# Matmul with bias and residual: groups of eight tiles in place of four, with one home for each residual group

## The chip, the cores and the metric

The kernel runs on one core of one Trainium2 chip. The metric is the device time of one execution in microseconds (us), the median of three runs. A profile is one more execution, read by a hardware profiler; its span leaves out a little at both ends of the device time.

## The reference

```python
x: 16 x 512 x 1024 f32, weight: 1024 x 768 f32, bias: 768 f32, residual: 16 x 512 x 768 f32
out = np.matmul(x, weight) + bias + residual        # f32
```

Flattened, it is 8192 rows of x, each times the whole weight. The kernel reads 33.6 MB of x, 25.2 MB of residual and 3.1 MB of weight and writes 25.2 MB, 87.04 MB in all.

## The kernel before, in words

**Tiles.** The 8192 rows are cut into 64 tiles of 128 rows. Four tiles (G = 4) are a group of 512 rows, which is loaded and stored with one DMA each. In `group`, partition p holds four consecutive rows of the group, so a partition's share of x is 16 KB in one piece, of residual and output 12 KB; tile j of the group takes row j of every partition. The weight is cut the same way, in two halves of 512 rows with four consecutive rows on a partition, and the strided view in `transpose` picks the columns of x that match.

**One tile's way.** ScalarE (ACT) casts the tile of x to bf16 (`cast_x`, L118; tiles 0 and 2 are shared out between ACT and VectorE, DVE: L115, L116). TensorE (PE) transposes it with eight matmuls against an identity into PSUM (`transpose`, L134). DVE copies the result to SBUF (`copy_xt`, L141). PE multiplies it with the bf16 weight in 16 matmuls, for each of eight k one of 512 and one of 256 columns (`matmul`, L148). `evacuate` ends it: in the first three groups (LATE = 3) DVE adds the bias into an output tile (L163) and GpSimd (POOL) the residual (L164); later DVE adds the product to the residual tile in place (L167) and POOL the bias (L169), and the residual tile is what is stored. The last group's bias is added ahead of time, half on DVE and half on POOL (`add_bias`, L177). The last tile is done in two column chunks (L275, L278).

**Buffers.** Four x slots of 16 KB a partition; a ring of nine slots of 12 KB that the two weight halves, the residual groups and the three output groups take in turn; four slots each for the cast x (`xb`) and the transposed x (`xt`); two PSUM slots for the transposes and three for the products. A load into a slot waits until the last reader of what it held is done; where a residual slot was stored from, it waits for that store to land.

**Order.** Every engine works in the order of the program text (`tc.keep_in_program_order`), and so does SP's queue, which issues all loads and stores (L90, L95, L99, L103): while one waits, all behind it wait. A DMA also waits for the one eight places before it to land, as eight completion semaphores are used in turn. The DMAs in flight share the core's 16 DMA engines and land in the order of issue.

**Start.** SP loads x rows 0 and 1 of the first group, w0, x rows 2 and 3, and the other weight pieces; then x groups 1 and 2, residual 0, x group 3, residuals 1 to 3. PE runs filler matmuls (`fill`, L201) while it waits. Tiles 0 to 2 are multiplied with each k of the weight as it arrives and is cast (`cast_w`, L123 on ACT, L125 on DVE); the bias is spread over the partitions (L212, `stream_shuffle`) before the first of these casts; tile 3 is transposed meanwhile. Its matmuls open the loop over tiles 3 to 62, in which PE transposes tile t + 1 ahead of the matmuls of tile t, and ACT casts tile t + 3. After the fourth tile of each group the loop loads x and residual four groups ahead and stores the group.

Of the kernel before, what the change touches and what calls it, by code (L numbers as in the profile page):

```python
# [8 lines left out]
FP32 = mybir.dt.float32  # L9
BF16 = mybir.dt.bfloat16  # L10
P = 128
G = 4
X_BUFS = 4
RING = 9
XB_BUFS = 4
XT_BUFS = 4
PT_BUFS = 2
PO_BUFS = 3
LATE = 3


@with_exitstack
def kernel(
# [8 lines left out]
    nc = tc.nc  # L32
# [4 lines left out]
    N = weight.shape[1]  # L37
    n_k = K // P
    n_sub = M // P
    n_grp = n_sub // G  # L40
    chunks = [(0, 512), (512, N - 512)]

    def group(ap, g):

        return ap[g * G * P:(g + 1) * G * P, :].rearrange("(p j) k -> p j k", p=P)


    w_dram = weight.rearrange("(h p j) n -> h p j n", p=P, j=4)
# [3 lines left out]
    ring_pool = ctx.enter_context(tc.tile_pool(name="ring", bufs=1))  # L52
# [7 lines left out]
    def o(ins):  # L60
        return tc.keep_in_program_order(ins)
# [3 lines left out]
    def slot(pool, base, n, shape, dtype, name=None):  # L65
        i = count.get(base, 0)
        count[base] = i + 1
        return pool.tile(shape, dtype, name=name or base, tag=f"{base}{i % n}", bufs=1)
# [4 lines left out]
    bias_rows = const.tile([P, N], FP32, name="bias_rows")  # L73
# [7 lines left out]
    w_sb = const.tile([P, n_k, N], BF16, name="w_sb")  # L81
    bias_bc = const.tile([P, N], FP32, name="bias_bc")


    x_tiles, r_tiles, o_tiles, w_stage = {}, {}, {}, {}

    def load_x(g, j0=0, j1=G):
        if g not in x_tiles:
            x_tiles[g] = slot(xin_pool, "x_tile", X_BUFS, [P, G, K], FP32)
        o(nc.sync.dma_start(out=x_tiles[g][:, j0:j1, :], in_=group(x2d, g)[:, j0:j1, :]))  # L90

    def load_w(h, j0, j1):
        if h not in w_stage:
            w_stage[h] = slot(ring_pool, "ring", RING, [P, G, N], FP32, name="w_stage")
        o(nc.sync.dma_start(out=w_stage[h][:, j0:j1, :], in_=w_dram[h, :, j0:j1, :]))  # L95

    def load_r(g):
        r_tiles[g] = slot(ring_pool, "ring", RING, [P, G, N], FP32, name="r_tile")
        o(nc.sync.dma_start(out=r_tiles[g], in_=group(res2d, g)))  # L99

    def store(g, j0=0, j1=G, n0=0, n1=N):
        src = o_tiles[g] if g < LATE else r_tiles[g]
        o(nc.sync.dma_start(out=group(out2d, g)[:, j0:j1, n0:n1], in_=src[:, j0:j1, n0:n1]))  # L103


    xb_tiles, pt_tiles, xt_tiles, po_tiles = {}, {}, {}, {}

    def cast_x(t, split=False):
        if t >= n_sub:
            return  # L110
        xb_tiles[t] = slot(xb_pool, "xb", XB_BUFS, [P, K], BF16)
        src = x_tiles[t // G][:, t % G, :]
        if split:
            h = K // 2
            o(nc.scalar.copy(out=xb_tiles[t][:, :h], in_=src[:, :h]))  # L115
            o(nc.vector.tensor_copy(out=xb_tiles[t][:, h:], in_=src[:, h:]))  # L116
        else:
            o(nc.scalar.copy(out=xb_tiles[t], in_=src))  # L118

    def cast_w(k, act=False):  # L120
        h, j = divmod(k, 4)
        if act:
            o(nc.scalar.copy(out=w_sb[:, k, :], in_=w_stage[h][:, j, :]))  # L123
        else:
            o(nc.vector.tensor_copy(out=w_sb[:, k, :], in_=w_stage[h][:, j, :]))  # L125

    def transpose(t):
        if t >= n_sub:
            return
        xb = xb_tiles.pop(t).rearrange("m (h p j) -> m h j p", p=P, j=4)  # L130
        pt = slot(pt_pool, "pt", PT_BUFS, [P, n_k, P], BF16)
        for k in range(n_k):
            h, j = divmod(k, 4)
            o(nc.tensor.transpose(out=pt[:, k, :], in_=xb[:, h, j, :], identity=ident))  # L134
        pt_tiles[t] = pt

    def copy_xt(t):
        if t >= n_sub:
            return
        xt_tiles[t] = slot(xt_pool, "xt", XT_BUFS, [P, n_k, P], BF16)  # L140
        o(nc.vector.tensor_copy(out=xt_tiles[t], in_=pt_tiles.pop(t)))  # L141

    def matmul(t, k0=0, k1=n_k):
        if t not in po_tiles:
            po_tiles[t] = slot(po_pool, "po", PO_BUFS, [P, N], FP32)
        for k in range(k0, k1):
            for (n0, nl) in chunks:
                o(nc.tensor.matmul(  # L148
                    po_tiles[t][:, n0:n0 + nl],
                    lhsT=xt_tiles[t][:, k, :],  # L150
                    rhs=w_sb[:, k, n0:n0 + nl],
                    start=(k == 0),
                    stop=(k == n_k - 1),
                ))

    def evacuate(t):
        g, j = divmod(t, G)
        po = po_tiles[t]
        if g < LATE:
            if g not in o_tiles:  # L160
                o_tiles[g] = slot(ring_pool, "ring", RING, [P, G, N], FP32, name="o_tile")
            ot = o_tiles[g]
            o(nc.vector.tensor_add(out=ot[:, j, :], in0=po, in1=bias_bc))  # L163
            o(nc.gpsimd.tensor_add(out=ot[:, j, :], in0=ot[:, j, :], in1=r_tiles[g][:, j, :]))  # L164
        else:
            rt = r_tiles[g][:, j, :]
            o(nc.vector.tensor_add(out=rt, in0=po, in1=rt))  # L167
            if g < n_grp - 1:
                o(nc.gpsimd.tensor_add(out=rt, in0=rt, in1=bias_bc))  # L169
        po_tiles.pop(t)  # L170
        xt_tiles.pop(t)

    def add_bias(t):
        g, j = divmod(t, G)
        rt = r_tiles[g]
        engine = nc.gpsimd if j % 2 else nc.vector
        o(engine.tensor_add(out=rt[:, j, :], in0=rt[:, j, :], in1=bias_bc))  # L177


    load_x(0, 0, 2)  # L180
    load_w(0, 0, 1)
    load_x(0, 2, 4)
    load_w(0, 1, 2)
    load_w(0, 2, 4)
    load_w(1, 0, 2)
    load_w(1, 2, 3)
    load_w(1, 3, 4)
    load_x(1)
    load_x(2)
    load_r(0)  # L190
    load_x(3)
    load_r(1)
    load_r(2)
    load_r(3)


    warm_ps = po_pool.tile([P, P], FP32, name="warm_ps", tag="po2", bufs=1)
# [1 line left out]
    def fill(n):  # L199
        for i in range(n):  # L200
            o(nc.tensor.matmul(warm_ps, lhsT=warm_in, rhs=warm_in, start=True, stop=True))  # L201
# [2 lines left out]
    fill(40)  # L204
    cast_x(0, True)
    transpose(0)
    fill(10)
    copy_xt(0)
    cast_x(1)
    transpose(1)  # L210
    fill(6)
    o(nc.vector.stream_shuffle(out=bias_bc, in_=bias_rows, mask=[0] * 32))  # L212
    cast_w(0)
    matmul(0, 0, 1)
    copy_xt(1)
    fill(4)
    matmul(1, 0, 1)
    cast_x(2, True)
    transpose(2)
    cast_w(1)  # L220
    copy_xt(2)
    matmul(0, 1, 2)
    matmul(1, 1, 2)
    matmul(2, 0, 2)
    cast_x(3)
    transpose(3)
    copy_xt(3)
    for k in range(2, 6):
        cast_w(k, k % 2 == 0)
        for t in range(3):  # L230
            matmul(t, k, k + 1)
    cast_w(6)
    cast_w(7, True)
    matmul(0, 6, 7)
    matmul(1, 6, 7)
    matmul(0, 7, 8)
    evacuate(0)
    matmul(2, 6, 8)
    matmul(1, 7, 8)
    evacuate(2)  # L240
    evacuate(1)
    cast_x(4)
    cast_x(5)


    for t in range(3, n_sub - 1):
        g, j = divmod(t, G)
        cast_x(t + 3)
        if t == 3:
            matmul(t)  # L250
            transpose(t + 1)
        else:
            transpose(t + 1)
            matmul(t)
        copy_xt(t + 1)
        evacuate(t)
        if g == n_grp - 2 and j >= 2:
            add_bias(n_sub - G + 2 * (j - 2))
            add_bias(n_sub - G + 2 * (j - 2) + 1)
        if j == G - 1:  # L260
            if g + 4 < n_grp:
                load_x(g + 4)
                load_r(g + 4)
            store(g)
        elif g == n_grp - 1 and j == 1:
            store(g, 0, 2)
        elif g == n_grp - 1 and j == 2:
            store(g, 2, 3)


    t = n_sub - 1
    for (n0, nl) in chunks:
# [4 lines left out]
        rt = r_tiles[n_grp - 1][:, G - 1, n0:n0 + nl]  # L277
# [30 lines left out]
```

## Time and profile before

| | us |
|---|---|
| three runs | 212.57, 212.7, 213.39; median 212.7 |
| the profiled execution | 212.85 |
| its span | 211.1 |
| PE busy (matmuls) | 202.3 (96%) |
| POOL busy | 114.5 (54%) |
| DVE busy | 107.0 (51%) |
| ACT busy | 66.0 (31%) |
| SP's DMA queue | packets take 97.9% of what 16 engines have |

How to read it. The span is that of the profiled execution; 212.85 less 211.1 is what lies around it. A busy share is of the span. The page cuts the span into 40 slices of 5.3 us and gives a digit for each engine, the busy share in tenths. The chain of waits goes back from the last instruction to what released it, and is listed in order of time as start, duration, what. A line of the timeline has start, duration, engine, source line, operation, output <- inputs, shape, count, and in brackets the idle time before it and what ended it.

### The profile page before, as it was taken

Reading aid. Unit: us, or ns where it says so; the run is one execution under the profiler, and the core shown is the slowest. Engines: PE = TensorE matmul, PEld = TensorE weight load, DVE = VectorE, ACT = ScalarE, POOL = GpSimd, SP = SyncE. Lnnn points to the kernel's source line nnn. Section 1 sums busy time; section 2 is a strip of 40 time slices with the busy share of each in tenths; the row PEclk is TensorE's granted clock in tenths of the full one; section 3 lists DMA queues with packets and bytes.
Section 4 is the critical chain, followed back from the end, with each engine's and each line's share of the span. In section 5 each row is a group of like instructions: output and inputs, shape, how many; then the busy total and the mean of one; then the engine's idle time right before and its main releaser. Section 6 shows DMA issues by size and latency. Waiting matters only on the chain.

```text
span 211.1 us, 3768 instructions
## 1 busy us (share of the span) xinstructions
PE 202.3 (96%) x1596; PEld 134.7 (64%) x1596; DVE 107.0 (51%) x142; ACT 66.0 (31%) x69; POOL 114.5 (54%) x69
## 2 busy tenths in 40 slices
PE   8599799999999999999999999999999999999992
PEld 7455466666666666666666666666666666666551
DVE  0664454554455445544554554455445544555942
ACT  2441772312507042150705225070430606033000
POOL 2000019699865565566556655665565566557910
PEclk9999999999999999999999999999999999999999
DMA  6999999999999999999999999999999999999895
GB/s 216 421 436 420 425 432 420 422 438 415 434 412 427 432 425 432 422 434 420 425 428 426 437 417 437 422 425 428 426 432 425 432 420 429 435 419 432 354 416 194
DMA packets 8377, 87.29 MB, mean 414 GB/s; under 512 B 932, under 2 KB 1060, under 8 KB 2216
## 3 DMA queue, kind: packets, MB, share of 16 engines
q1 hardware_dynamic: 8352, 87.04, 97.9%
q8 instruction: 12, 0.20, 0.4%
q14 instruction: 5, 0.04, 0.0%
q10 hardware_dynamic: 8, 0.01, 0.0%
HBM read 61.88 MB, written 25.17 MB: 412 GB/s over the span
## 4 chain that ended last, share of the span: by engine, by line
PE 85%; DMA 10%; DVE 2%; issue 1%; ACT 1%; POOL 0%; ACTq 0%; DVEq 0%; POOLq 0%
PE po L148 72%; PE pt L134 12%; DMA x_tile<-in_x_dram 7%; DMA bias_rows<-in_bias_dram 3%; PE last_ps L275 1%; DVE r_tile L177 1%; ACT xb L118 1%; DVE xt L141 0%; DVE r_tile L278 0%; POOL ident masks.py:197 0%; ACTq L118 0%; POOL bias_rows L74 0%; DVE r_tile L167 0%; DVEq L167 0%; POOLq L292 0%
## 5 line engine op out<-in xcount | busy, mean ns | idle before, releaser
L148 PE MATMUL po<-w_sb,xt 128*128 128x512 bf16 x1008 | 174.6, 326 | 1.2 <-DVE w_sb L125 0.8
L148 PEld LDWEIGHTS <-xt 128*128 128x128 bf16 x1008 | 95.9, 98 | 59.4 <-issue 1.6
L169 POOL TENSOR_TENSOR r_tile<-r_tile,bias_bc 128x768 f32<-128x768 f32 x48 | 88.3, 1840 | 56.0 <-DVE r_tile L167 56.0
L118 ACT CAST xb<-x_tile 128x1024 bf16<-128x1024 f32 x62 | 61.0, 1043 | 115.2 <-DMA x_tile<-in_x_dram 109.2
L167 DVE TENSOR_TENSOR r_tile<-po,r_tile 128x768 f32<-128x768 f32 x51 | 48.8, 957 | 73.6 <-PE po L148 62.9
L141 DVE COPY xt<-pt 128x1024 bf16<-128x1024 bf16 x64 | 43.6, 681 | 4.9 <-PE pt L134 4.8
L134 PEld LDWEIGHTS <-xb 128*128 128x128 bf16 x512 | 35.4, 113 | 10.3 <-ACT xb L118 1.6
L134 PE MATMUL pt<-ident,xb 128*128 128x128 bf16 x512 | 39.1, 219 | 2.4 <-ACT xb L115 1.3
L164 POOL TENSOR_TENSOR o_tile<-o_tile,r_tile 128x768 f32<-128x768 f32 x12 | 21.4, 1822 | 30.3 <-DMA r_tile<-in_residual_dram 30.3
L163 DVE TENSOR_TENSOR o_tile<-po,bias_bc 128x768 f32<-128x768 f32 x12 | 11.3, 955 | 14.5 <-PE po L148 13.0
L201 PE MATMUL warm_ps<-warm_in 128*128 128x128 bf16 x60 | 6.1, 282 | 1.1 <-DVE warm L77 1.1
L201 PEld LDWEIGHTS <-warm_in 128*128 128x128 bf16 x60 | 5.5, 132 | 1.2 <-DVE warm L77 1.1
L123 ACT CAST w_sb<-w_stage 128x768 bf16<-128x768 f32 x3 | 2.5, 833 | 4.2 <-DMA w_stage<-in_weight_dram 4.2
L177 POOL TENSOR_TENSOR r_tile<-r_tile,bias_bc 128x768 f32<-128x768 f32 x2 | 3.6, 1804 | 0.0
L116 DVE CAST xb<-x_tile 128x512 bf16<-128x512 f32 x2 | 0.8, 423 | 5.2 <-DMA x_tile<-in_x_dram 5.2
L177 DVE TENSOR_TENSOR r_tile<-r_tile,bias_bc 128x768 f32<-128x768 f32 x2 | 3.1, 1551 | 0.0
L125 DVE CAST w_sb<-w_stage 128x768 bf16<-128x768 f32 x5 | 2.7, 556 | 0.5 <-DMA w_stage<-in_weight_dram 0.4
L275 PE MATMUL last_ps<-w_sb,xt 128*128 128x512 bf16 (+1 forms) x16 | 2.8, 326 | 0.0
L115 ACT CAST xb<-x_tile 128x512 bf16<-128x512 f32 x2 | 1.2, 618 | 3.9 <-DMA x_tile<-in_x_dram 3.9
L275 PEld LDWEIGHTS <-xt 128*128 128x128 bf16 x16 | 1.6, 98 | 1.1
L78 ACT ACT_TABLE_LOAD x1 | 1.3, 1283 | 2.6 <-POOL ident masks.py:199 2.6
L278 DVE TENSOR_TENSOR r_tile<-last_ps,r_tile 128x512 f32<-128x512 f32 (+1 forms) x2 | 1.1, 559 | 0.9 <-PE last_ps L275 0.8
(12 smaller groups left out, 3.1 us busy)
## 6 DMA issues: line engine op xcount, KB each, us to landing
x_tile<-in_x_dram SPq DMA_DIRECT2D x15, 2048.0 KB, 32.9
r_tile<-in_residual_dram SPq DMA_DIRECT2D x16, 1536.0 KB, 32.1
out_dram<-r_tile SPq DMA_DIRECT2D x12, 1536.0 KB, 31.7
out_dram<-o_tile SPq DMA_DIRECT2D x3, 1536.0 KB, 25.2
x_tile<-in_x_dram SPq DMA_DIRECT2D x2, 1024.0 KB, 6.7
w_stage<-in_weight_dram SPq DMA_DIRECT2D x4, 384.0 KB, 9.7
w_stage<-in_weight_dram SPq DMA_DIRECT2D x2, 768.0 KB, 10.2
out_dram<-r_tile SPq DMA_DIRECT2D x1, 768.0 KB, 5.6
```

The lines of the kernel that those rows point to most:

```text
L118: o(nc.scalar.copy(out=xb_tiles[t], in_=src))
L125: o(nc.vector.tensor_copy(out=w_sb[:, k, :], in_=w_stage[h][:, j, :]))
L134: o(nc.tensor.transpose(out=pt[:, k, :], in_=xb[:, h, j, :], identity=ident))
L141: o(nc.vector.tensor_copy(out=xt_tiles[t], in_=pt_tiles.pop(t)))
L148: o(nc.tensor.matmul(po_tiles[t][:, n0:n0 + nl], lhsT=xt_tiles[t][:, k, :], rhs=w_sb[:, k, n0:n0 + nl], start=(k == 0), stop=(k == n_k - 1),))
L163: o(nc.vector.tensor_add(out=ot[:, j, :], in0=po, in1=bias_bc))
L164: o(nc.gpsimd.tensor_add(out=ot[:, j, :], in0=ot[:, j, :], in1=r_tiles[g][:, j, :]))
L167: o(nc.vector.tensor_add(out=rt, in0=po, in1=rt))
L169: o(nc.gpsimd.tensor_add(out=rt, in0=rt, in1=bias_bc))
L177: o(engine.tensor_add(out=rt[:, j, :], in0=rt[:, j, :], in1=bias_bc))
L201: o(nc.tensor.matmul(warm_ps, lhsT=warm_in, rhs=warm_in, start=True, stop=True))
L275: o(nc.tensor.matmul(ps, lhsT=xt_tiles[t][:, k, :], rhs=w_sb[:, k, n0:n0 + nl], start=(k == 0), stop=(k == n_k - 1)))
```

## The change

- G is 8: one DMA serves eight tiles, and a partition's piece is 32 KB for x and 24 KB for residual and output. There are two x slots of 32 KB in place of four of 16 KB, and four slots of 24 KB (`home`) in place of nine of 12 KB. HOME names the slot of each residual group; slot 0 first holds the whole weight, slot 2 the output of group 0.
- Only group 0 has an output tile of its own, and its residual is loaded later; POOL adds that residual for all eight tiles in a row after tile 12 (`add_residual`). All other groups add in place.
- A table, `moves`, says after which tile SP issues which load and store. The residual and store of a group come later than before, and each x load two groups ahead.
- The start: the first x group comes in five pieces (rows 0-1, 2, 3, 4-5, 6-7), the last three behind the weight, which comes in seven. Tile 2 is cast by ACT alone, tile 3 by ACT and DVE together after the weight; its transposes come after the matmuls of tiles 0 to 2. The bias is spread after the cast of w5. Fills are 40, 8 and 6 in place of 40, 10, 6 and 4. There are five `xb` slots.
- In the loop, tile 3's matmuls are parted by the transposes of tile 4, and tile 7's come before the transposes of tile 8.
- At the end, tiles 61 to 63 get their bias on DVE beforehand, one a tile at tiles 57 to 59; the others up to 60 on POOL after their own add. The last group is stored in pieces of four, two and one tiles and the two chunks of the last tile.

```diff
--- before.py
+++ after.py
@@ -9,14 +9,13 @@
 FP32 = mybir.dt.float32
 BF16 = mybir.dt.bfloat16
 P = 128
-G = 4
-X_BUFS = 4
-RING = 9
-XB_BUFS = 4
+G = 8
+X_BUFS = 2
+HOME = [3, 1, 0, 3, 1, 2, 0, 3]
+XB_BUFS = 5
 XT_BUFS = 4
 PT_BUFS = 2
 PO_BUFS = 3
-LATE = 3
 
 
 @with_exitstack
@@ -81,6 +80,9 @@
     w_sb = const.tile([P, n_k, N], BF16, name="w_sb")
     bias_bc = const.tile([P, N], FP32, name="bias_bc")
 
+    def home(i, name):
+        return ring_pool.tile([P, G, N], FP32, name=name, tag=f"ring{i}", bufs=1)
+
 
     x_tiles, r_tiles, o_tiles, w_stage = {}, {}, {}, {}
 
@@ -90,16 +92,17 @@
         o(nc.sync.dma_start(out=x_tiles[g][:, j0:j1, :], in_=group(x2d, g)[:, j0:j1, :]))
 
     def load_w(h, j0, j1):
-        if h not in w_stage:
-            w_stage[h] = slot(ring_pool, "ring", RING, [P, G, N], FP32, name="w_stage")
-        o(nc.sync.dma_start(out=w_stage[h][:, j0:j1, :], in_=w_dram[h, :, j0:j1, :]))
+        if not w_stage:
+            w_stage[0] = home(0, "w_stage")
+        o(nc.sync.dma_start(out=w_stage[0][:, 4 * h + j0:4 * h + j1, :],
+                            in_=w_dram[h, :, j0:j1, :]))
 
     def load_r(g):
-        r_tiles[g] = slot(ring_pool, "ring", RING, [P, G, N], FP32, name="r_tile")
+        r_tiles[g] = home(HOME[g], "r_tile")
         o(nc.sync.dma_start(out=r_tiles[g], in_=group(res2d, g)))
 
     def store(g, j0=0, j1=G, n0=0, n1=N):
-        src = o_tiles[g] if g < LATE else r_tiles[g]
+        src = o_tiles[g] if g == 0 else r_tiles[g]
         o(nc.sync.dma_start(out=group(out2d, g)[:, j0:j1, n0:n1], in_=src[:, j0:j1, n0:n1]))
 
 
@@ -118,11 +121,10 @@
             o(nc.scalar.copy(out=xb_tiles[t], in_=src))
 
     def cast_w(k, act=False):
-        h, j = divmod(k, 4)
         if act:
-            o(nc.scalar.copy(out=w_sb[:, k, :], in_=w_stage[h][:, j, :]))
+            o(nc.scalar.copy(out=w_sb[:, k, :], in_=w_stage[0][:, k, :]))
         else:
-            o(nc.vector.tensor_copy(out=w_sb[:, k, :], in_=w_stage[h][:, j, :]))
+            o(nc.vector.tensor_copy(out=w_sb[:, k, :], in_=w_stage[0][:, k, :]))
 
     def transpose(t):
         if t >= n_sub:
@@ -154,44 +156,43 @@
                 ))
 
     def evacuate(t):
+
+
         g, j = divmod(t, G)
-        po = po_tiles[t]
-        if g < LATE:
-            if g not in o_tiles:
-                o_tiles[g] = slot(ring_pool, "ring", RING, [P, G, N], FP32, name="o_tile")
-            ot = o_tiles[g]
-            o(nc.vector.tensor_add(out=ot[:, j, :], in0=po, in1=bias_bc))
-            o(nc.gpsimd.tensor_add(out=ot[:, j, :], in0=ot[:, j, :], in1=r_tiles[g][:, j, :]))
+        po = po_tiles.pop(t)
+        if g == 0:
+            o(nc.vector.tensor_add(out=o_tiles[0][:, j, :], in0=po, in1=bias_bc))
         else:
             rt = r_tiles[g][:, j, :]
             o(nc.vector.tensor_add(out=rt, in0=po, in1=rt))
-            if g < n_grp - 1:
-                o(nc.gpsimd.tensor_add(out=rt, in0=rt, in1=bias_bc))
-        po_tiles.pop(t)
+            if t < n_sub - 3:
+                add_bias(t)
         xt_tiles.pop(t)
 
-    def add_bias(t):
-        g, j = divmod(t, G)
-        rt = r_tiles[g]
-        engine = nc.gpsimd if j % 2 else nc.vector
-        o(engine.tensor_add(out=rt[:, j, :], in0=rt[:, j, :], in1=bias_bc))
+    def add_bias(t, engine=nc.gpsimd):
+        rt = r_tiles[t // G][:, t % G, :]
+        o(engine.tensor_add(out=rt, in0=rt, in1=bias_bc))
+
+    def add_residual(t):
+        ot = o_tiles[0][:, t, :]
+        o(nc.gpsimd.tensor_add(out=ot, in0=ot, in1=r_tiles[0][:, t, :]))
 
 
     load_x(0, 0, 2)
     load_w(0, 0, 1)
-    load_x(0, 2, 4)
+    load_x(0, 2, 3)
     load_w(0, 1, 2)
-    load_w(0, 2, 4)
-    load_w(1, 0, 2)
-    load_w(1, 2, 3)
-    load_w(1, 3, 4)
+    load_w(0, 2, 3)
+    load_w(0, 3, 4)
+    load_w(1, 0, 1)
+    load_w(1, 1, 2)
+    load_w(1, 2, 4)
+    load_x(0, 3, 4)
+    load_x(0, 4, 6)
+    load_x(0, 6, 8)
     load_x(1)
-    load_x(2)
-    load_r(0)
-    load_x(3)
     load_r(1)
-    load_r(2)
-    load_r(3)
+    o_tiles[0] = home(2, "o_tile")
 
 
     warm_ps = po_pool.tile([P, P], FP32, name="warm_ps", tag="po2", bufs=1)
@@ -204,68 +205,82 @@
     fill(40)
     cast_x(0, True)
     transpose(0)
-    fill(10)
+    fill(8)
     copy_xt(0)
     cast_x(1)
+    cast_w(0)
     transpose(1)
+    copy_xt(1)
     fill(6)
-    o(nc.vector.stream_shuffle(out=bias_bc, in_=bias_rows, mask=[0] * 32))
-    cast_w(0)
     matmul(0, 0, 1)
-    copy_xt(1)
-    fill(4)
     matmul(1, 0, 1)
-    cast_x(2, True)
+    cast_x(2)
+    cast_w(1)
     transpose(2)
-    cast_w(1)
     copy_xt(2)
     matmul(0, 1, 2)
     matmul(1, 1, 2)
     matmul(2, 0, 2)
-    cast_x(3)
-    transpose(3)
-    copy_xt(3)
     for k in range(2, 6):
         cast_w(k, k % 2 == 0)
         for t in range(3):
             matmul(t, k, k + 1)
+    o(nc.vector.stream_shuffle(out=bias_bc, in_=bias_rows, mask=[0] * 32))
     cast_w(6)
     cast_w(7, True)
-    matmul(0, 6, 7)
-    matmul(1, 6, 7)
-    matmul(0, 7, 8)
+    cast_x(3, True)
+    matmul(0, 6, 8)
     evacuate(0)
+    matmul(1, 6, 8)
     matmul(2, 6, 8)
-    matmul(1, 7, 8)
+    transpose(3)
+    copy_xt(3)
+    evacuate(1)
     evacuate(2)
-    evacuate(1)
     cast_x(4)
     cast_x(5)
 
 
+    moves = {
+        4: [(load_x, 2)],
+        5: [(load_r, 0), (load_r, 2)],
+        12: [(load_x, 3), (load_r, 3)],
+        15: [(store, 1)],
+        20: [(load_x, 4)],
+        21: [(load_r, 4), (store, 0)],
+        28: [(load_x, 5)],
+        29: [(load_r, 5), (store, 2)],
+        36: [(load_x, 6)],
+        37: [(load_r, 6), (store, 3)],
+        44: [(load_x, 7)],
+        45: [(load_r, 7), (store, 4)],
+        47: [(store, 5)],
+        55: [(store, 6)],
+        59: [(store, 7, 0, 4)],
+        61: [(store, 7, 4, 6)],
+        62: [(store, 7, 6, 7)],
+    }
     for t in range(3, n_sub - 1):
-        g, j = divmod(t, G)
         cast_x(t + 3)
         if t == 3:
+            matmul(t, 0, 5)
+            transpose(t + 1)
+            matmul(t, 5, 8)
+        elif t == G - 1:
             matmul(t)
             transpose(t + 1)
         else:
             transpose(t + 1)
             matmul(t)
         copy_xt(t + 1)
+        if n_sub - 7 <= t < n_sub - 4:
+            add_bias(t + 4, nc.vector)
         evacuate(t)
-        if g == n_grp - 2 and j >= 2:
-            add_bias(n_sub - G + 2 * (j - 2))
-            add_bias(n_sub - G + 2 * (j - 2) + 1)
-        if j == G - 1:
-            if g + 4 < n_grp:
-                load_x(g + 4)
-                load_r(g + 4)
-            store(g)
-        elif g == n_grp - 1 and j == 1:
-            store(g, 0, 2)
-        elif g == n_grp - 1 and j == 2:
-            store(g, 2, 3)
+        if t == 12:
+            for u in range(G):
+                add_residual(u)
+        for move, *what in moves.get(t, []):
+            move(*what)
 
 
     t = n_sub - 1
```

## The prediction

> **What bounds the kernel now.** I read the page's slices first, then the chain that ended last, then the timeline of the start and the end, then the landings of single transfers. The slices say that two things are full at once:
>
> ```profile
> PE   8599799999999999999999999999999999999992
> DMA  6999999999999999999999999999999999999895
> PEclk9999999999999999999999999999999999999999
> q1 hardware_dynamic: 8352, 87.04, 97.9%
> PE 85%; DMA 10%; DVE 2%; issue 1%; ACT 1%; POOL 0%; ACTq 0%; DVEq 0%; POOLq 0%
> ```
>
> TensorE and the DMA engines are both at 9 tenths from the second slice to the last but one, at a granted clock of 0.999. The chain of waits tells which ends last:
>
> ```profile
> 21.93 0.04 ACTq L118
> ...
> 24.06 0.64 PE pt L134 x8
> 24.70 2.61 PE po L148 x16
> 27.31 0.45 PE pt L134 x8
> 27.75 2.60 PE po L148 x16
> ...
> 195.79 2.15 DVE r_tile L177
> 197.94 0.61 DVE xt L141
> ...
> 204.42 2.61 PE last_ps L275 x16
> 207.06 0.42 DVE r_tile L278
> ```
>
> From 24.06 on it is TensorE alone, 0.45 + 2.60 us a tile, a period of 3.048 us (tile 5's transposes at 24.06, tile 6's at 27.31, tile 8's matmuls ending at 39.5). Before that the chain is in the second x load, which holds ACT's casts until 22. After PE's end at 207.04 come one add, the last store (issued 207.51, landed 210.0) and the end at 211.07: a tail of 4.03 us. So the time is PE's start, 60 tiles at a fixed pace, and the tail.
>
> The transfers are barely quicker than that. The landings recorded for single transfers step by 4.85 us for 2048 KB of x, 3.66 for a residual, 3.70 for a store: 12.2 us for four tiles, where PE takes 4 x 3.048 = 12.19. The slack of x late in the run:
>
> ```profile
> 188.12 3.89 ACT L118 CAST xb<-x_tile 128x1024 bf16<-128x1024 f32 x4 [8.32 <-DMA x_tile<-in_x_dram]
> ...
> 191.66 0.61 PE L134 MATMUL pt<-ident,xb 128*128 128x128 bf16 x8
> ```
>
> ACT starts the casts of the last group when x lands, and PE transposes the first of these tiles 3.5 us later. The changed kernel must therefore shorten PE's path and must not let the DMA queue run dry by more than a few us.
>
> **The transfers, part by part.** By the recorded packets, 12288 B take 460 ns on an engine (median), 16384 B 611, 6144 B 234, 3072 B 121: 0.0369 ns a byte and 7 to 8 ns a packet. Bytes stay at 87.04 MB. Data packets fall from about 7420 to 4990 (x rows of 32 KB, residual and store rows of 24 KB, but the first x group in five pieces and w in seven), so 2430/16 x 7.4 ns = 1.1 us less for each engine. No row has a 32 KB packet: if packets are cut back to 16 KB and 12 KB it is 0; if all per-packet cost went, 7420/16 x 7.4 = 3.4 us. I take 1.1, since four sizes lie on one line. By it eight tiles take 9.7 + 7.3 + 7.4 = 24.4 us at most, PE 24.38. Nothing of it lies on the path of PE; it moves the end only if the queue ends last.
>
> The Trainium skill's page "DMA: Bandwidth & Descriptors", Anatomy of one DMA, gives a fixed 2.0 us for each DMA beside bytes/436 GB/s; by it 22 DMAs fewer would save up to 44 us, but 1536 KB landing every 3.66 us leaves no room for a fixed part, so I use nothing of it. The same page, Latency and other measured facts, speaks against wide power-of-two pitches (207 GB/s at a row pitch of 512 KiB, 164 at 2 MiB); no run here shows one, x at 16 KB pitch moves at 16 x 16384/611 = 429 GB/s, no slower than 12 KB rows at 427, and the sum has no term for it.
>
> **The start.** The order on SP becomes x rows 0-1, w0, x row 2, w1 to w5, w6-7, then x row 3, 4-5, 6-7, x group 1, residual 1. Up to w6-7 this is 0.52 MB less ahead of the last weights (1.2 us by the 2.4 us between the landings of the first and second 1024 KB of x). Landings, stepping by the same rates from the shown 6.13 (first x): w0 7.2, x row 2 8.4, w1 9.4, w2 10.3, w3 11.3, w4 12.3, w5 13.2, w6-7 15.1. Before shows a slip of 0.8 us at the last weight piece (15.30 to 17.05 for 384 KB, where 0.96 is usual), which I spread: w6-7 15.1 to 15.9, x row 3 16.3 to 17.1, rows 4-5 18.8 to 19.5, rows 6-7 21.2 to 21.9. x group 1 lands at 31.6 and residual 1 at 38.9; these bytes are those of before's 39.27.
>
> PE then: the weight casts (0.56 DVE, 0.83 ACT) end by 16.0 to 16.7, the last two k of tiles 0 to 2 are 12 matmuls of 0.163 = 1.95, to 18.3 (middle). Transposes of tile 3 and copy_xt(3), 0.45 + 0.2 + 0.69, to 19.6; ten matmuls 1.63, tile 4's transposes 0.45, six matmuls 0.98: tile 3 ends at 22.7. Tiles 4 to 6 at 3.05 each: 31.8. Tile 7 is put ahead of tile 8's transposes, as x group 1 lands only at 31.6: 34.4. Then two transposes, a bare wait for copy_xt(8) of 0.45 and 2.6: tile 8 ends at 38.4, 0.75 to 1.45 around it. Before has it at 39.5. **Gain 1.1 us.** The bias spread (1.01 us of DVE), moved from ahead of cast_w(0) to behind w5's cast, is hidden there by the wait for w6-7; without that cover it would cost its 1.0. The fills dropped (6 of 60) run only where PE waits.
>
> **The steady part.** SP's queue is in order, so a waiting instruction holds all behind it. With PE's tile t ending at 38.4 + 3.048(t-8), step by step:
> - x2 waits for the cast of tile 7 (about 24); r0 and r2 follow at once. The queue is full to then. Landings: x2 48.6, r0 55.9, r2 63.2. Tile 16 ends at 62.8, so its add waits 0.4 us; copy_xt(18) behind it on DVE ends at 65.0, needed at 66.3. Residual 1 at 38.9 against tile 8 at 38.4 likewise.
> - x3 waits for the cast of tile 15, which the fifth xb buffer allows at about 38.5: lands 72.9.
> - r3 goes into residual 0's slot, so it waits for eight residual adds that POOL does in a row from 55.9, 1.785 each (10.70/6): 70.3. Behind it on SP wait store 1 and x4. The packets of x3 end at about 71.9 and an issue takes about 1.0 us to its first packet (0.74 to 1.73 at the start): **margin 0.6 us**, no gap. POOL's bias adds of tiles 13 to 15 queue behind: store 1 at 75.9, no gap (r3 lands 80.2).
> - r4 waits for store 1's landing (87.6), r5 for store 0 (112.0), r6 for store 2 (136.4), r7 for store 3 (160.8), each with the next x still 9.7 us in the queue ahead or behind it. x4 to x7 land at 97.3, 121.7, 146.1, 170.5 and are needed at tiles 31, 39, 47, 55, 8 us later; r4 to r7 land 6.8 us ahead.
> So PE is nowhere held; cost 0. By the ledger the queue ends at 207.4; with the two slips of 0.6 and 0.9 us that before's landings show (at 150.8 and 167.4), 208.9 at worst. PE's path has its last store land at 210.0 - 1.2 = 208.8.
>
> **The end.** Three bias adds go to DVE (tiles 61 to 63) where before had two on DVE and two more on POOL.
>
> ```profile
> 195.32 1.81 POOL L177 TENSOR_TENSOR r_tile<-r_tile,bias_bc 128x768 f32<-128x768 f32 x1
> 195.79 2.15 DVE L177 TENSOR_TENSOR r_tile<-r_tile,bias_bc 128x768 f32<-128x768 f32 x1
> ```
>
> A DVE add with two SBUF inputs took 0.95 alone and 2.15 beside a POOL add (it ended 0.81 after POOL did). Three such in three tiles, each waiting for POOL's add, push copy_xt(61) to about 0.15 us past its need; before lost 0.25 there. Bounds: 0 to 0.9 (one more blocked add, 2.15 less 1.25). Gain 0.1.
>
> **Sum.** 212.85 (the profiled execution: span 211.1 and 1.8 around it) - 1.1 - 0.1 = 211.65; the median shown lies 0.15 lower, so **211.5**, its own range 210.6 (1.45 at the start, no stall at the end) to 212.2.
>
> **Rivals.** *The queue ends last*: packets of 32 KB are no cheaper, or the slips are larger. For: the queue's end and PE's are within 0.2 us of each other, and 1.1 us of saving is an extrapolation. Against: 2.97 us of idle, a mean of the 16 engines, between before's first and last packet. Price: queue end 208.9 + 1.1 = 210.0, so 212.7: no change. *SP stands at r3*: POOL's eight residual adds are slower, or residual 0 lands late; the queue drains at 72 with store 1 and x4 stuck behind r3. For: POOL adds of 2.46 and 2.53 stand in the last 20 us of the trace, and residual groups have no slot to spare. Against: those were beside DVE adds of two SBUF inputs, which group 1 has none of. At 2.5 each it is 8 x 0.715 = 5.7 us, less the margin 0.6: the queue ends at 207.4 + 5.1 + 1.5 = 214, 5.2 past PE's store: 216.7. It makes the kernel slower than before once the adds are late by 0.6 + 1.1 = 1.7 us or more (queue end 208.9 against before's 210.0); 2.5 us late gives 212.7 + 0.8 = 213.5. *The start gains nothing*: tile 3, now alone behind the weights, waits for a late x row 3, 1.2 us more: 212.7.
>
> **How the numbers follow.** The forecast 0.50, the queue or the start without gain 0.32, SP at r3 0.18. Something over 0.5% (211.64 to 213.76 around the median) is what a measurement can tell. Most of the forecast's own range lies on the faster side (0.42 of 0.50) and a better packet saving cannot add much, as PE's path stays: faster 0.45; within 0.5% 0.37 (the rest, the second case and a little of the third); slower 0.18. The range leaves out the dearer part of the third case: 210.5 to 214.0.
>
> **What would show it.** Right: tile 8's matmuls end near 38.4; PE's last matmul near 205.8; periods of 3.048 with no gaps at tiles 16, 24, 32; r3 issued near 70 with no drop in the DMA slices there; packets of 32 KB near 1215 ns. Wrong: a dip in the DMA slices at 70 to 76, ACT's casts ending at need at tile 32 or later, a last store that lands long after the last add, or DVE adds of tile 61 to 63 that hold copy_xt by more than 1 us.

## The result

| | median us | runs | range |
|---|---|---|---|
| before | 212.97 | 20 | 212.57 to 213.74 |
| after | 214.03 | 20 | 212.59 to 215.08 |

The ratio after to before is 1.0044, 95% interval 1.0023 to 1.0064: slower by 0.9 us by this ratio (the medians differ by 1.06), where 211.5 was forecast. The times of after are spread over twice the range of before's. The profiled execution of after took 214.12 us, its span is 212.3.

**The profile after.** The page's slices, queue and chain:

```profile
PE   7797999999999999999999999999999999999960
...
PEclk9999999999999999999999999999999999999997
DMA  6999999999999899999999999999999999999993
GB/s 234 405 420 435 482 411 423 448 404 417 435 420 468 324 347 392 448 420 432 431 440 445 411 425 415 445 428 418 440 440 443 401 445 429 423 426 438 408 413 120
...
q1 hardware_dynamic: 5616, 87.03, 97.3%
...
PE 87%; DMA 7%; issue 1%; DVE 1%; ACT 0%; SPq 0%; POOL 0%; POOLq 0%
```

A third of the packets is gone (5616 for 8352), as meant: the data packets among them fall from 7424 to 4992. PE now has nothing to do in the last slice, while DMA is still at 3 tenths: the end has changed hands. And in the slices 14 to 16 (69 to 85 us) the rate falls to 324, 347 and 392 GB/s, although the DMA digit falls only once, to 8. Before has 432, 425 and 432 there:

```profile
GB/s 216 421 436 420 425 432 420 422 438 415 434 412 427 432 425 432 422 434 420 425 428 426 437 417 437 422 425 428 426 432 425 432 420 429 435 419 432 354 416 194
```

The end of the chain of waits after:

```profile
200.05 2.60 PE po L150 x16
202.65 2.61 PE last_ps L290 x16
205.26 0.02 issue
205.29 0.42 DVE r_tile L293
```

PE's last matmul ends at 205.26, before 207.04: PE's path became 1.8 us shorter in this execution. But this chain stops at the last compute instruction. The landing of the last store stands in the list of DMA issues, whose last column is the time from issue to landing. Before, then after:

```profile
out_dram<-r_tile SPq DMA_DIRECT2D x1, 128.0 KB, 2.5
```

```profile
out_dram<-r_tile SPq DMA_DIRECT2D x1, 384.0 KB, 6.8
out_dram<-r_tile SPq DMA_DIRECT2D x1, 256.0 KB, 6.0
out_dram<-r_tile SPq DMA_DIRECT2D x1, 128.0 KB, 5.7
```

Before's last store, 128 KB, landed 2.5 us after its issue, after's 5.7: issued at 205.74, it lands at 211.44. It stood behind other stores. The DMA queue ends last, not PE.

**Where the queue lost time.** SP's part of the timeline of after (start, duration, line, what):

```profile
39.74 0.33 SPq L92 DMA_DIRECT2D x_tile<-in_x_dram  x1
70.58 0.33 SPq L102 DMA_DIRECT2D r_tile<-in_residual_dram  x1
75.91 0.35 SPq L106 DMA_DIRECT2D out_dram<-r_tile  x1
76.35 0.38 SPq L92 DMA_DIRECT2D x_tile<-in_x_dram  x1
```

and the waits of SP's queue:

```profile
SPq L102 <- POOL o_tile L178: 14.3, 1, 14.3
```

From 39.74 to 70.58 SP issues nothing; at the last it stands for 14.3 us at residual 3, for the residual adds of POOL. What it issued then came 2.7 us before x group 3, the last transfer in the queue, had landed (73.27). Residual 3 landed at 83.85, 10.6 us behind x group 3; the other residuals whose landing is recorded take 7.3 to 7.5. After that the steps are again 7.3 and 9.7, but for two slips of 0.6 and 0.8 us, as before had two. The windows view of after at this place (busy time of each engine, then the granted clock, the DMA share and GB/s):

```profile
63.00:71.00 8.00, 7.89 (x59) 5.22 (x60) 4.57 (x6) 1.04 (x1) 8.00 (x6) 1.00 0.93 396
71.00:80.00 9.00, 8.95 (x72) 6.00 (x72) 4.66 (x6) 4.93 (x5) 9.00 (x6) 1.00 1.00 337
80.00:89.00 9.00, 8.89 (x71) 5.94 (x71) 4.66 (x6) 3.14 (x3) 9.00 (x6) 1.00 1.00 424
```

From 71 to 80 the DMA share is 1.00 and the rate 337 GB/s: the engines are not idle, their packets are slow. The recorded packets say which. A packet of 24 KB usually takes 912 ns. On one engine, residual 3 (eight packets) runs 1990, 910, 910, 910, 910, 1010, 2120, 980 ns. Most engines show this: the first packet takes 1.4 to 2.0 us where the engine had run dry before it; on nearly all the seventh takes 1.6 to 2.2, and the sixth or the eighth some tenths too long. Four engines never ran dry, and their eight packets still took 1.5 us over the usual time, the others' 1.9 to 3.0. As a mean of the 16 engines that is 2.0 us, and only 0.3 us of idle. On the slowest engine it is 3.0 us, and a transfer lands with its slowest engine: the step was 3.3 us over the usual.

### The profile page after: what moved, and what is told of

Same layout as the page of the kernel before. It is cut to its first block, busy times and chain, and to the rows that moved or that the text cites. A ratio compares the mean times of both kernels' runs of the same rounds, so it can differ in the third digit from the quotient of the medians.

```text
span 212.3 us, 3674 instructions
## 1 busy us (share of the span) xinstructions
PE 199.6 (94%) x1560; PEld 133.8 (63%) x1590; DVE 110.3 (52%) x143; ACT 66.7 (31%) x69; POOL 111.0 (52%) x68
## 3 DMA queue, kind: packets, MB, share of 16 engines
q1 hardware_dynamic: 5616, 87.03, 97.3%
## 4 chain that ended last, share of the span: by engine, by line
PE 87%; DMA 7%; issue 1%; DVE 1%; ACT 0%; SPq 0%; POOL 0%; POOLq 0%
PE po L150 73%; PE pt L136 13%; DMA x_tile<-in_x_dram 4%; DMA bias_rows<-in_bias_dram 3%; PE last_ps L290 1%; DVE xt L143 1%; ACT xb L118 0%; DVE r_tile L293 0%; SPq L97 0%; POOL ident masks.py:197 0%; POOL bias_rows L73 0%; POOLq L307 0%
## 5 line engine op out<-in xcount | busy, mean ns | idle before, releaser
L150 PE MATMUL po<-w_sb,xt 128*128 128x512 bf16 (+1 forms) x978 | 172.2, 324 | 3.2 <-DVE xt L143 1.5
L174 POOL TENSOR_TENSOR r_tile<-r_tile,bias_bc 128x768 f32<-128x768 f32 x53 | 95.5, 1816 | 85.1 <-DVE r_tile L167 85.0
L167 DVE TENSOR_TENSOR r_tile<-po,r_tile 128x768 f32<-128x768 f32 x55 | 52.6, 956 | 76.1 <-PE po L150 65.8
L178 POOL TENSOR_TENSOR o_tile<-o_tile,r_tile 128x768 f32<-128x768 f32 x8 | 14.2, 1820 | 3.1 <-DMA r_tile<-in_residual_dram 3.1
L164 DVE TENSOR_TENSOR o_tile<-po,bias_bc 128x768 f32<-128x768 f32 x8 | 7.5, 952 | 4.8 <-PE po L150 4.8
L174 DVE TENSOR_TENSOR r_tile<-r_tile,bias_bc 128x768 f32<-128x768 f32 x3 | 6.6, 2188 | 0.0
L202 PE MATMUL warm_ps<-warm_in 128*128 128x128 bf16 x54 | 5.1, 275 | 1.1 <-DVE warm L76 1.1
L202 PEld LDWEIGHTS <-warm_in 128*128 128x128 bf16 x54 | 4.7, 129 | 1.0 <-DVE warm L76 1.0
L228 DVE STREAM_SHUFFLE bias_bc<-bias_rows 128x768 f32<-128x768 f32 x1 | 1.0, 1012 | 0.0
```

The lines of the kernel that those rows point to most:

```text
L150: o(nc.tensor.matmul(po_tiles[t][:, n0:n0 + nl], lhsT=xt_tiles[t][:, k, :], rhs=w_sb[:, k, n0:n0 + nl], start=(k == 0), stop=(k == n_k - 1),))
L164: o(nc.vector.tensor_add(out=o_tiles[0][:, j, :], in0=po, in1=bias_bc))
L174: o(engine.tensor_add(out=rt, in0=rt, in1=bias_bc))
L178: o(nc.gpsimd.tensor_add(out=ot, in0=ot, in1=r_tiles[0][:, t, :]))
```

## The experiments

Theory Q: the queue must not only be busy when residual 3 is issued, it must hold several us of work, or the refill costs packets of double length; this put the end on the queue. Rival P: the wide packets, or engines that fall behind, are slow by themselves. Rival R: what costs is the lateness of residual 3, or POOL's adds beside it. Times of an experiment are compared with before runs on the same chip; before's median was 212.89 for the first four kernels and 212.76 for the other three.

**e1: residual 0 is loaded early**, so POOL's adds start early and residual 3 is issued early.

```diff
     load_r(1)
+    load_r(0)
...
-        5: [(load_r, 0), (load_r, 2)],
+        5: [(load_r, 2)],
```

> Only the load of residual 0 moves: from after tile 5 to the start, behind residual 1, so that POOL's eight residual adds no longer wait for it and residual 3 is issued at about 67.5 us in place of 70.6, some 5 us before the x load ahead of it is through. Theory Q (the DMA queue runs dry ahead of residual 3, and filling it again costs more than the gap): residual 3 lands 7.3 us after x group 3, not 10.6; the queue ends 3.3 us earlier, PE's path ends last, time about 211.2 us. Rival P (the wide packets or single engines that fall behind are slow by themselves, wherever the loads stand): the step stays near 10 us and the time near 214.

211.77 us (211.50 to 212.14), ratio to before 0.9948 (0.9933 to 0.9962). Q holds, P falls: the packets are as wide and the loss is gone but for a rest. Residual 3 was issued at 68.67, 4.9 us ahead of x group 3's landing at 73.55, and landed 7.9 us behind it, 0.6 over the usual. On most engines one packet is slow, mostly the seventh at 1.1 to 1.7 us; on two it is the first, at 1.9. No engine ran dry. The SP timeline and the window of e1:

```profile
68.67 0.33 SPq L102 DMA_DIRECT2D r_tile<-in_residual_dram  x1
```

```profile
71.00:80.00 9.00, 8.90 (x71) 6.00 (x72) 4.52 (x7) 4.20 (x5) 9.00 (x6) 1.00 0.99 397
```

PE's end came at 206.78 in place of 205.26, which I had not foreseen. I put that down to x group 2, which now stands behind residual 0 and landed at 56.5; e5 was made for it, and showed that it was something else.

**e2: POOL's residual adds later** (after tile 14), so that residual 3 is issued later but store 1 as before.

```diff
-        if t == 12:
+        if t == 14:
```

> The changed kernel with POOL's residual adds put after tile 14 in place of 12, so that residual 3 is issued about 3.2 us later (73.8) while store 1, which waits for POOL's bias add of tile 15, comes at the same 75.9. Theory Q: the queue is empty for 2 us before residual 3, and the time grows by about what the issue is late, to 216 to 217.5 us. Rival P: within 0.5 of the changed kernel.

216.60 us (215.36 to 217.08), ratio 1.0164 (1.0139 to 1.0190). Residual 3 was issued at 74.75, 4.2 us after the changed kernel's (3.2 were expected), and the queue was empty for 4.2 us (mean of the engines). The windows view of e2:

```profile
71.00:80.00 9.00, 8.95 (x71) 6.03 (x72) 4.53 (x7) 4.40 (x5) 9.00 (x7) 1.00 0.53 195
```

Here the DMA share falls with the rate, to 0.53. On top of the gap come the same slow packets, 2.0 us as a mean of the engines. So a later issue costs the gap, and the refill costs its own price whether or not there is a gap.

**e3: e1, with POOL's residual adds earlier too** (after tile 9).

```diff
-        if t == 12:
+        if t == 9:
```

> As e1, and POOL's residual adds after tile 9 in place of 12, so that residual 3 is issued at about 61 us, 11 us before x group 3 is through. Theory Q: nothing is left to gain over e1 (within 0.4 us, about 211.2), and no slow packets of residual 3. If 5 us of lead are too few, e3 is quicker than e1 and shows how much lead is wanted. Rival P: near 214 as e1.

211.76 us (211.47 to 211.85), ratio 0.9945 (0.9932 to 0.9957). Residual 3 was issued at 60.90 and landed 7.3 us after x group 3; no slow packets. The time is e1's; PE's end is late here too (206.53).

**e4: e1, with every DMA of eight tiles cut in two**, so that packets are 16 and 12 KB.

```diff
 def load_x(g, j0=0, j1=G):
+    if j1 - j0 == G:
+        load_x(g, 0, 4)
+        load_x(g, 4, 8)
+        return
```

and likewise in `load_r` and `store`.

> As e1, with every DMA of eight tiles cut into two of four rows a partition, so that packets are 16 KB and 12 KB as before the change: 2816 more packets, 176 on an engine, at 7.4 ns, and 23 more DMAs. Theory Q with the packet price of the prediction: 1.3 to 1.5 us more of DMA time than e1, so the queue ends at about 209.3 and the time is 0.5 to 1.2 us over e1. Rival: the packet size is worth nothing because PE's path ends last in both: within 0.3 us of e1. Rival P: clearly quicker than the changed kernel in any case, as the packets are narrow again.

212.78 us (212.51 to 213.25), ratio 0.9996 (0.9987 to 1.0005): 1.0 us more than e1, inside what was expected. The last store lands at 210.1, e1's at 209.3, though PE ends 0.9 us earlier than in e1 (205.88). So wide packets do not cost; they are worth about 1 us here. The queue may save more than that, as e4 did not have e1's rest of 0.6 us at residual 3: issued 5.8 us ahead, its two halves took 7.4 us and had no slow packets.

**e5: residual 0 between two halves of x group 2**, adds after tile 9, to have the lead without PE's wait.

```diff
-        4: [(load_x, 2)],
-        5: [(load_r, 0), (load_r, 2)],
+        4: [(load_x, 2, 0, 4), (load_r, 0), (load_x, 2, 4, 8)],
+        5: [(load_r, 2)],
...
-        if t == 12:
+        if t == 9:
```

> The changed kernel with x group 2 loaded in two halves and residual 0 between them, and POOL's residual adds after tile 9: residual 0 lands at about 51.4 in place of 56.2, residual 3 is issued at about 66, some 5 us before x group 3 is through, and x group 2's first tiles land at 44, so that PE does not wait for them as it did in e1 and e3 (chain: x group 2 landed 56.3, PE's end 206.5 to 206.8 in place of 205.3). Theory Q: residual 3's step near 7.3 us, PE's end near 205.3, the queue then ends last near 208; time 210.8 to 211.4, 0.4 to 1.0 under e1. If e1's loss on PE's path is not the late x group 2, e5 equals e1 (211.8).

211.85 us (211.17 to 212.84), ratio 0.9954 (0.9938 to 0.9969). That is the second branch, e1's time: x group 2 was not what e1 lost. In e5's profile residual 3 was issued at 65.84 with a step of 7.3, and PE did end at 205.54, but for another reason; its last store was issued at 206.02 and landed at 208.90, so there the queue ended last. PE's end goes with the casts of the last weight pieces on ACT, here in e1 and in the changed kernel:

```profile
16.44 0.83 ACT L125 CAST w_sb<-w_stage 128x768 bf16<-128x768 f32 x1 [3.65 <-DMA w_stage<-in_weight_dram]
```

```profile
14.64 0.83 ACT L125 CAST w_sb<-w_stage 128x768 bf16<-128x768 f32 x1 [2.02 <-DMA w_stage<-in_weight_dram]
```

Where these casts start at 16.0 to 16.4 (e1, e2, e3), PE ends at 206.5 to 206.8; where they start at 14.6 to 14.8 (after, e4, e5, e7), at 205.2 to 205.9. x group 2 holds PE by 0.2 us in e1 and 0.4 in e3. The loads up to there are the same in all seven kernels, and e2 is the changed kernel up to residual 3, so this is a difference between executions, not between kernels. Part of it goes with the order of w6-7 and an instruction load of 16 KB that one engine serves at about 14 us: in e1, e2 and e3 that engine is through with w6-7 1.0 to 1.4 us after all others; in after, e4, e5 and e7 all are through within 0.7 us, and it falls back only at a later transfer. The rest is open.

**e6: the new start alone**, in the kernel before.

```diff
-    load_x(0, 2, 4)
+    load_x(0, 2, 3)
     load_w(0, 1, 2)
-    load_w(0, 2, 4)
-    load_w(1, 0, 2)
...
+    load_w(1, 2, 4)
+    load_x(0, 3, 4)
+    load_x(1, 0, 2)
+    load_x(1, 2, 4)
```

and the order of casts, transposes and matmuls up to tile 3 as in the changed kernel.

> One part of the change alone: the kernel before, groups of four, with the new order of the first tiles (loads of x and weight in the new order and pieces, x group 1 in two pieces, tiles 0 to 3 as in the changed kernel). PE should be about 1.3 to 1.9 us further by tile 8 as in the changed kernel. If PE's path alone sets the end, as the prediction has it, the time falls by as much, to 211 to 211.5. If the queue with its narrow packets ends right behind it (before's slowest engine was through with store 12 at 202.2, and 7.4 us of stores follow), it falls by 0 to 0.5, to 212.4 to 212.9.

213.45 us (213.14 to 214.13), ratio 1.0033 (1.0023 to 1.0043): slower, outside both expectations. The page's chain of waits of e6:

```profile
DMA 85%; PE 5%; POOL 3%; SPq 2%; issue 1%; DVE 1%; DVEq 0%; POOLq 0%
```

The same chain in before had PE at 85%. In e6 tile 8's matmuls ended at 38.5, 1.0 us before before's, but the chain now runs through the queue. Near the end DVE, in program order, waits for the last residual and holds PE up:

```profile
192.55 1.98 DVE L177 TENSOR_TENSOR r_tile<-r_tile,bias_bc 128x768 f32<-128x768 f32 x1 [0.72 <-DMA r_tile<-in_residual_dram]
```

PE waits 0.86 us after it and ends at 206.68, 0.4 before before's. The last store lands at 210.79, before's at 210.0. That 0.8 is lost at the start: x group 2, behind the same bytes in both, landed at 27.80, before's at 26.81. More and smaller pieces (three more DMAs) are part of it; by the packet price they are 0.2, the rest I did not settle.

**e7: half of x group 4 ahead of residual 3**, whose issue stays where it was.

```diff
-        12: [(load_x, 3), (load_r, 3)],
-        15: [(store, 1)],
-        20: [(load_x, 4)],
+        12: [(load_x, 3)],
+        20: [(load_x, 4, 0, 4), (load_r, 3), (store, 1), (load_x, 4, 4, 8)],
```

> The changed kernel with the first half of x group 4 issued ahead of residual 3 and the second half behind store 1; residual 0 and POOL's adds stay, so residual 3 is issued at the same 70.6 us. Theory Q: the queue then holds 4.85 us more when residual 3 is issued, so no slow packets and no gap; x group 4's first half lands near 78, residual 3 near 85.4, in time for tile 24's add at 86; time as e5, 210.8 to 211.6. Rival R (what costs is that residual 3 comes late, or that POOL's adds run beside it, and not that the queue is empty): residual 3's step stays near 10 us and the time near 214.

211.51 us (211.27 to 212.34), ratio 0.9946 (0.9929 to 0.9963). The SP timeline and the window of e7:

```profile
64.04 0.33 SPq L92 DMA_DIRECT2D x_tile<-in_x_dram  x1
70.38 0.33 SPq L102 DMA_DIRECT2D r_tile<-in_residual_dram  x1
75.70 0.35 SPq L106 DMA_DIRECT2D out_dram<-r_tile  x1
```

```profile
71.00:80.00 9.00, 9.00 (x73) 6.04 (x72) 4.66 (x6) 4.93 (x5) 9.00 (x6) 1.00 1.02 435
```

Residual 3 is issued at the same time as in the changed kernel and lands later (85.75), POOL adds beside it as before, and the rate in the same nine us is 435 in place of 337. R falls. This is the quickest kernel here, by the median.

All six with groups of eight that load residual 3 whole, by the lead (landing of the transfer ahead of it less its issue), us:

| kernel | residual 3 issued | lead | step (7.3 usual) | slow packets, mean of engines |
|---|---|---|---|---|
| e2 | 74.75 | -1.2 | 12.6 | 2.0 |
| after | 70.58 | 2.7 | 10.6 | 2.0 |
| e1 | 68.67 | 4.9 | 7.9 | 0.6 |
| e5 | 65.84 | 7.6 | 7.3 | 0.0 |
| e7 | 70.38 | 8.0 | 7.3 | 0.1 |
| e3 | 60.90 | 12.5 | 7.3 | 0.0 |

Each row is one execution. A lead of 7.6 us is enough, 4.9 nearly.

## Why the prediction was wrong, step by step

- **Packets: right.** 32 KB took 1213 ns and 24 KB 912, against 1215 and 913 by the line through the four sizes. e4, with 176 more packets on an engine, should cost 1.3 us by that line and came 1.0 dearer than e1.
- **The start: right in this execution, partly by luck.** x group 1 landed at 31.7 (31.6), residual 1 at 39.2 (38.9); tile 8's matmuls ended at 38.1 (38.4). But in e2, the same program up to there, they ended at 39.3: of the 1.4 us gained here, 0.2 was left.
- **The end on PE's side: right.** PE ended at 205.26 (205.8), 0.4 us gained behind tile 8 where 0.1 was forecast. The three bias adds on DVE took 2188 ns each; PE was not held:

```profile
L174 DVE TENSOR_TENSOR r_tile<-r_tile,bias_bc 128x768 f32<-128x768 f32 x3 | 6.6, 2188 | 0.0
```

- **x and residuals in time: right.** The last x group's casts start where x lands, and PE needs the first of its tiles 3.8 us later (before 3.5; 8 were forecast, and the loss at residual 3 took most of the rest):

```profile
174.33 5.78 ACT L121 CAST xb<-x_tile 128x1024 bf16<-128x1024 f32 x6 [12.75 <-DMA x_tile<-in_x_dram]
...
178.11 0.61 PE L136 MATMUL pt<-ident,xb 128*128 128x128 bf16 x8
```

- **The step that failed: "margin 0.6 us, no gap".** The issue came when forecast (70.58 for 70.3), store 1 too (75.91 for 75.9), and there was hardly a gap (0.3 us, as x group 3 ended between 71.0 and 73.2 on the engines, not at 71.9 on all). But I priced an issue by its time to the first packet alone, 1.0 us, and took any margin over it as free. The sum had nothing for what followed: the first packet of an engine that had run dry, and the seventh of nearly every engine, took one and a half to two and a half times as long. That was 2.0 us as a mean of the engines, 3.0 on the slowest, 3.3 at the landing. e1, e3, e5 and e7 took the time back by issuing earlier or by putting work ahead of it. This was in before's trace to be seen: its 8 KB packets took 352 ns in the mean and 309 in the median, and the slow ones are the first packets of its first transfer, where the queue starts empty.
- **The rival "SP stands at r3" had the place and not the cause.** It asked for slower adds on POOL. They took 1820 ns, close to the forecast (8 of 1.785), and residual 3 was 0.3 us late; the queue lost 3.3.
- **The rival "the queue ends last" had the right path and another cause.** Packets of 32 KB were as cheap as hoped. Against it stood 2.97 us of idle between before's first and last packet; by the page's 97.9%, with 1.7 us ahead of the first and 1.4 behind the last, it was 1.3. The queue had less to spare than the prediction said.
- **What bounds the kernel was read too simply.** That "it is TensorE alone" held for before by little: its last store of 128 KB took 2.5 us to land, e3's 1.8, so some 0.7 us of before's tail was already the queue's (an estimate from these two). In e6 a PE path that was 1.0 us ahead at tile 8 gained nothing, and the chain went from 85% PE to 85% DMA. The ledger's queue end, 207.4 to 208.9, becomes 210.7 to 212.2 with the 3.3 us; it was 211.4.
- With the refill gone the forecast's 211.5 is what e7 measures (211.51); that is the sum's size met by one kernel, not the forecast, which was of the change. The parts differ: e7's PE ended at 205.19, 1.85 us before before's and not 1.2, and the span ended 4.48 us after it and not 4.03, as the queue still ended last.
- Smaller slips: PE's second slice is at 5 and its fifth at 7 tenths, so TensorE is not full from the second on; the DMAs saved are 19 (59 to 40), not 22. No term of the sum rests on either. And the 2.0 us a DMA that the prediction quotes is, on that page of the Trainium skill, a fit to DMAs issued by GpSimd, where this kernel's loads and stores come from SP; the sum used nothing of it.

The wider spread of after's times (2.5 us, e7 1.1) would fit a kernel whose queue is refilled at the edge in every execution, with a start that comes 1.3 us earlier or later; no run was made to show that.

## What to carry to other kernels

Where the DMA queue is full from end to end, ask of each issue how many us of work are still queued ahead of it, not whether it arrives before the queue is dry; here 4.9 us were nearly enough, and 5.8 (e4, in halves) and 7.6 were. A slot that frees late at the head of an in-order queue takes that lead from everything behind it: put a transfer that is free to go (here half of a later x group) ahead of the wait. And a chain of waits that ends at the last compute instruction doesn't see the queue: compare the last store's time to landing before and after.

## What the runs showed that I had not expected

- A full DMA share is no full rate: 1.00 at 337 GB/s (after, 71 to 80 us) and 1.02 at 435 (e7, the same stretch). Why it is the first and then mainly the seventh (in e2 the seventh and eighth) of the residual's eight packets that are slow is open; store 1 was issued 2 to 3 us ahead of the seventh packets in after (75.91) and 5 us or more in e2 (76.54), so it is not that nothing stood behind.
- The 16 engines drift apart, and a transfer lands with the slowest. In after the spread of their completions grows from 0.4 us in the first transfer to 4.2 at store 4. Part of it has a visible cause: each of 12 instruction loads of 16 KB took some 1.0 us of one engine, and after the one at 14.0 us the slowest engine's completion falls 1.1 us back (15.45 for the last but one, 16.54 for the last). In before the others waited at 199 to 200 us for store 14, and the spread shrank to 1.7; after's queue never paused, and of its last 3.6 us the engines were idle for 2.3 in the mean while the late ones finished.
